# Prompt attention with the keys on partitions: transposed scores 512 queries wide, and no transposes of P

## The chip, the cores and the metric

The kernel runs on one core of one Trainium2 chip. A core has five engines that run side by side, each with an instruction queue of its own that it works off in order: TensorE (PE) for matrix products, VectorE (DVE), ScalarE (ACT), GpSimd (POOL) and SyncE (SP), which issues nearly all DMAs here. A program set the order in each queue when the kernel was built. The metric is the time of one execution on the device in microseconds (us), lower is better.

## The reference

One inference step of a one-layer streaming encoder. 1168 rows go through every dense product: 128 new rows of eight running streams (16 each, with 512 cached rows), and a prompt of 16 learned meta tokens and 1024 frames. Two attentions run in parallel on the same input, a forgetting attention (below: Fox) and a latent one (MLA), 8 heads each; a gated merge and a convolutional feed-forward part follow. What matters here is the attention of the prompt:

```
def attend(q, k, v, bias, scale):
    s = jnp.einsum('bqhd,bkhd->bhqk', q, k).astype(jnp.float32) * scale + bias
    p = jax.nn.softmax(s, axis=-1).astype(v.dtype)
    return jnp.einsum('bhqk,bkhd->bqhd', p, v)
...
fox_bias:  jnp.where(causal, Fq[..., None] - F[:, :, None, :], NEG)   # F: running sum of the log forget values
mla_bias:  cid = jnp.where(idx < N_META, 0, 1 + (idx - N_META) // CHUNK)   # CHUNK = 64
           jnp.where((cid[None, :] <= cq[:, None]) & key_ok[None, :], 0.0, NEG)
```

So for each of 16 heads there are 1024 queries and 1040 keys, causal for Fox and causal by chunks of 64 for MLA. All of it is in float32.

## The kernel before

A float32 product is made of products of two reduced parts: a number x is held as `h` (x rounded to the matrix format, an ACT copy) and `l` (x minus h, a DVE subtraction); the helper `split` (line 293) is this pair of instructions. A dense product takes three matmuls (hh, hl, lh).

The program has these stages in time: projections of all rows; the attention of the running streams; **the attention of the prompt (`sweep`, line 1070)**, from 555 to 943 us of the profiled execution; the merge and the output projection; the feed-forward part, from 1108 us to the end.

In `sweep` a unit is one head and two blocks of 128 queries. Queries are on partitions. `fronts` (line 960) makes the scores of a block in pieces of up to 456 keys, in banks of PSUM named `sb` (two of them). Fox takes two matmuls a piece: high and low parts of k lie one above the other on 128 partitions, q's high part (twice) and low part are the weights. MLA takes three. A bf16 matmul with the identity adds the causal mask `trib` for Fox. `evac_min` (line 667) is one DVE instruction that adds the bias, writes the score to SBUF (`S`) and keeps the row's minimum (scores are negated, so this is softmax's maximum). ACT then takes exp of the row and its sum (line 989), DVE the reciprocal of the sum, one number per query (lines 993 to 1001), and POOL scales the row (lines 994 to 1004).

`backs` (line 1008) turns P around: `lift` puts 128x128 pieces of P through PE transposes into `tb`, `split` brings them to SBUF as `ph` and `pl`, and `pv` multiplies them with V, 256 queries wide, into `ob`. The 16 meta keys are a product of their own (`pm` and `vm`). `finish` adds the two halves of `ob` and stores the head's output (`of`) to DRAM.

`sweep` writes the order of PE out by hand (`emit`, with each piece pinned): the fronts of the next units and pieces of other dense work (`slices`: the gates in Fox, the output projection of Fox in MLA, in banks `mmb`) are spread between the pieces of the present unit. The other queues follow from program order. SBUF tiles for a head's keys and queries are loaded one head ahead, each tile with two buffers.

Of the kernel before, what the change touches and what calls it, by code (L numbers as in the profile page):

```python
# [19 lines left out]
P = 128  # L20
D = 1024
KT = 8
NSMP = 128
# [45 lines left out]
def build(ctx, nc, tc, a):  # L69
# [25 lines left out]
    VF, VM = scratch("VF", [8, P, 1024]), scratch("VM", [8, P, 1024])  # L95
    VZF, VZM = scratch("VZF", [64, 2, 1024]), scratch("VZM", [64, 2, 1024])
# [177 lines left out]
    tri32 = const("tri", [P, P])  # L274
    c16 = const("c16", [P, 16])
    dma(VZF, a["zv"])
    dma(VZM, a["zv"])
    idb = cp.tile([P, P], BF16, name="idb")
    trib = cp.tile([P, P], BF16, name="trib")
    dve.tensor_copy(idb, ident)  # L280
    dve.tensor_copy(trib, tri32)
# [25 lines left out]

    def put_meta(Z, cs, src):
        z4 = Z.rearrange("(g w r) x c -> w x r g c", g=2, w=2)
        for w in range(2):  # L310
            store(z4[w, w][:, :, cs], src.unsqueeze(1).to_broadcast([16, 2, src.shape[-1]]))
# [20 lines left out]
    def fv_tile(i):  # L332
# [14 lines left out]
        put_meta(VZF, cs, f(vmt).rearrange("p h t d -> p (h t d)"))  # L347
        for jq in range(2):
# [7 lines left out]
            store(VF[4 * jq:4 + 4 * jq, :, cs].rearrange("j p c -> p j c"),  # L356
# [76 lines left out]
    with tc.tile_pool(name="rk", bufs=1, side="right") as rk:  # L433
# [37 lines left out]
        for j, (t0, tn) in enumerate(toks[1:]):  # L471
# [11 lines left out]
            if j:  # L483
                store(VM[j - 1], vhl)
            else:
                put_meta(VZM, slice(0, 1024), vhl)

    with tc.tile_pool(name="rm", bufs=1, side="right") as rm:
# [60 lines left out]
        store(FPR, no)  # L549
        ls = rm.tile([64, NK], F32, name="ls")  # L550
# [361 lines left out]
    def head_tiles(kind, h):  # L912
        t = {}
        hs = slice(64 * h, 64 * h + 64)
        fox = kind == 0
        np_ = P if fox else 96
        k1 = pp.tile([np_, NP], F32R, tag="k1", name="k1", padded_shape=[P, NP])
        q1 = pp.tile([np_, NF_], F32R, tag="q1", name="q1", padded_shape=[P, NF_])
        q2 = pp.tile([np_, NF_], F32R, tag="q2", name="q2", padded_shape=[P, NF_])
        if fox:  # L920
            dma(f(k1[0:64]), KFH[hs])
            dma(f(k1[64:128]), KFL[hs])
            for e in range(2):
                dma(f(q1[64 * e:64 * e + 64]), QH[hs])
                dma(f(q2[64 * e:64 * e + 64]), QL[hs])
            fb = pp.tile([P, NP], F32, tag="x", name="fb", padded_shape=[P, NP])
            dma(fb, FPR[h:h + 1, :].to_broadcast([P, NP]))
            t["fb"] = fb
        else:
# [78 lines left out]
    def backs(kind, h, s, t, SS):  # L1008
# [5 lines left out]
        def lift(jp):  # L1014
            def go():
# [11 lines left out]
                if last:  # L1027
                    pe.transpose(tb[0:32, col:col + P], SS[:, 0:32], ident)
# [476 lines left out]
```

## Time and profile before

| | |
|---|---|
| time, median of 3 runs | 1974.3 us (1972.53 to 1976.03) |
| the profiled execution: its own time | 1977.4 us |
| its span in the trace | 1975.6 us |
| span of the prompt's attention | 555 to 943 us |
| mean granted clock of TensorE | 0.993 |

The profile was taken from one execution by the hardware. It gives each instruction's start and duration on its engine, and for idle time the event that ended it. PE's durations overlap, since matmuls are pipelined and their ends are modelled; what one matmul costs in a row is the distance between two starts. DVE's durations overlap a little too: the next instruction's start is about 0.08 us ahead of the end of the one before.

### The profile page before, as it was taken

The page shows a single profiled execution, that of the slowest core. Times are in us where ns is not written, and L with a number is a line of the kernel's source. Part 1 is how long each engine was busy: PE and PEld are TensorE (multiplying, and loading weights), DVE is VectorE, ACT ScalarE, POOL GpSimd, SP SyncE. Part 2 cuts the span into 40 slices and gives each one's busy share as a digit, 9 for nine tenths or more (in the row PEclk, how much of TensorE's full clock was granted, in tenths as well). Part 3 has the DMA queues.
Part 4 walks back from the last instruction along what each step waited for, and adds up shares of the span by engine and source line. Part 5 has one row for each costly group of instructions (what it writes and reads, how often), then busy time and mean ns, then how long its engine had stood idle before and what let it go on. Part 6 is the DMA issues. An engine that isn't in the chain of part 4 may idle for free.

```text
span 1975.6 us, 30184 instructions
## 1 busy us (share of the span) xinstructions
PE 1926.9 (98%) x11766; PEld 1855.5 (94%) x11766; DVE 1125.4 (57%) x2118; ACT 700.0 (35%) x1182; POOL 333.2 (17%) x508
## 2 busy tenths in 40 slices
PE   8999999998999999999999999999999999999997
PEld 7999988988889898999899999999999999999996
DVE  7345355332547777666863465555645655645567
ACT  6222132122446667666632231121221221221235
POOL 5110000111123333333312200000000000000024
PEclk9999999998999999999999999999999999999999
DMA  5345346795576565551733511111111111111112
GB/s 177 115 156 200 132 182 221 243 313 161 180 180 174 143 150 146 123 121 38 243 135 132 185 43 43 43 43 34 42 44 43 43 43 43 34 42 43 43 41 98
DMA packets 112824, 228.07 MB, mean 115 GB/s; under 512 B 12738, under 2 KB 66402, under 8 KB 111626
## 3 DMA queue, kind: packets, MB, share of 16 engines
q1 hardware_dynamic: 112138, 225.62, 37.0%
q8 instruction: 93, 1.52, 0.3%
q10 hardware_dynamic: 544, 0.52, 0.1%
q14 instruction: 49, 0.40, 0.1%
HBM read 165.87 MB, written 61.12 MB: 115 GB/s over the span
## 4 chain that ended last, share of the span: by engine, by line
PE 85%; DVE 6%; DMA 4%; ACT 2%; issue 2%; SPq 1%; POOL 1%; DVEq 0%; ACTq 0%; POOLq 0%
PE nb L63 59%; PE mmb L63 9%; PE ob L63 6%; PE sb L63 6%; PE tb L66 4%; DVE res L1377 1%; PE tb L63 1%; DMA gb<-GL 1%; DVE S L669 1%; DMA wr<-w_a 1%; DMA craw<-cckvT 1%; DVE ga L1189 0%; POOL ss L243 0%; DVE res L1280 0%; DVE zl L295 0%
## 5 line engine op out<-in xcount | busy, mean ns | idle before, releaser
L160 ACT ACTIVATE wh<-wr 128x1024 fp32r<-128x1024 f32 (+3 forms) x131 | 128.5, 981 | 725.2 <-PE nb L63 629.0
L63 PE MATMUL nb<-yl,wh 128*128 128x390 f32 (+1 forms) x1056 | 359.6, 341 | 0.0
L63 PE MATMUL nb<-yh,wl 128*128 128x390 f32 (+1 forms) x1056 | 358.8, 340 | 0.0
L63 PE MATMUL nb<-yh,wh 128*128 128x390 f32 (+1 forms) x1056 | 358.6, 340 | 0.0
L63 PEld LDWEIGHTS nb<-yh,wh 128*128 128x128 f32 x1056 | 199.2, 189 | 0.5
L63 PEld LDWEIGHTS nb<-yl,wh 128*128 128x128 f32 x1056 | 198.8, 188 | 0.4
L63 PEld LDWEIGHTS nb<-yh,wl 128*128 128x128 f32 x1056 | 198.7, 188 | 0.0
L63 PE MATMUL nb<-hh,wh 128*128 128x390 f32 (+2 forms) x552 | 184.3, 334 | 0.0
L63 PE MATMUL nb<-hl,wh 128*128 128x390 f32 (+2 forms) x552 | 183.6, 333 | 0.3 <-DVE hl L295 0.3
L63 PE MATMUL nb<-hh,wl 128*128 128x390 f32 (+2 forms) x552 | 183.5, 332 | 0.0
L1280 DVE TENSOR_TENSOR res<-nb,res 128x390 f32<-128x390 f32 (+3 forms) x260 | 137.2, 547 | 69.1 <-PE nb L63 68.5
L63 PE MATMUL nb<-xh,wh 128*128 128x390 f32 (+1 forms) x480 | 166.3, 346 | 5.4 <-ACT wh L160 5.4
L1261 DVE TENSOR_TENSOR up<-nb,rb 128x390 f32<-128x390 f32 x88 | 49.4, 562 | 205.0 <-PE nb L63 205.0
L63 PE MATMUL nb<-xh,wl 128*128 128x390 f32 (+1 forms) x480 | 164.8, 343 | 0.6 <-DVE wl L161 0.6
L63 PE MATMUL nb<-xl,wh 128*128 128x390 f32 (+1 forms) x480 | 163.7, 341 | 0.2 <-DVE xl L230 0.2
L161 DVE TENSOR_TENSOR wl<-wr,wh 128x1024 fp32r<-128x1024 f32 (+2 forms) x107 | 127.5, 1191 | 45.9 <-ACT wh L160 45.5
L63 PE MATMUL sb<-k,q 96*128 96x456 f32 (+17 forms) x560 | 141.6, 351 | 4.3 <-DVE mx L669 2.7
L295 DVE TENSOR_TENSOR pl<-tb,ph 128x512 fp32r<-128x512 f32 (+1 forms) x160 | 101.5, 634 | 27.6 <-ACT ph L294 25.4
L989 ACT ACTIVATE S<-S,mx 128x400 f32<-128x400 f32 (+7 forms) x128 | 100.5, 786 | 42.5 <-DVE mx L669 41.5
L63 PE MATMUL mmb<-xh,wh 128*128 128x390 f32 (+1 forms) x312 | 110.9, 355 | 0.0
L63 PE MATMUL mmb<-xh,wl 128*128 128x390 f32 (+1 forms) x312 | 106.7, 342 | 1.3 <-POOL wl L161 1.3
L294 ACT ACTIVATE ph<-tb 128x512 fp32r<-128x512 f32 (+1 forms) x160 | 88.1, 551 | 52.1 <-PE tb L66 49.7
(314 smaller groups left out, 4023.9 us busy)
## 6 DMA issues: line engine op xcount, KB each, us to landing
wr<-w_up SPq DMA_DIRECT2D x44, 512.0 KB
wr<-w_a SPq DMA_DIRECT2D x28, 512.0 KB
wr<-w_down SPq DMA_DIRECT2D x22, 512.0 KB
krw<-ckT SPq DMA_DIRECT2D x8, 1024.0 KB
vr<-cv SPq DMA_DIRECT2D x8, 1024.0 KB
GL<-gl SPq DMA_DIRECT2D x26, 195.0 KB
ga<-GL SPq DMA_DIRECT2D x8, 584.0 KB
gb<-GL SPq DMA_DIRECT2D x8, 584.0 KB
```

Of the source, the lines that this page charges most:

```text
L63: return self._put(self.eng.matmul(*args, **kw))
L66: return self._put(self.eng.transpose(*args, **kw))
L160: act.activation(wh[:, sl], wr[:, sl], AF.Copy)
L161: (eng or dve).tensor_tensor(wl[:, sl], wr[:, sl], f(wh[:, sl]), ALU.subtract)
L294: act.activation(hi, src, AF.Copy)
L295: (eng or dve).tensor_tensor(lo, src, f(hi), ALU.subtract)
L669: dve.tensor_tensor_reduce(out=S[:, c0:c1], in0=ps, in1=bias, scale=1.0, scalar=(3.0e38 if prev is None else prev), op0=ALU.add, op1=ALU.m ...
L989: act.activation(S[:, :n], S[:, :n], AF.Exp, bias=mn["m"], scale=-1.0, accum_out=rs[:, i % 2:i % 2 + 1])
L1261: dve.tensor_tensor(up[:, 18 + c0:18 + c1], ps, rb2[:, c0:c1], ALU.mult)
L1280: pin(dve.tensor_tensor(res[:, m, d0:d1], ps, res[:, m, d0:d1], ALU.add))
L1377: pin(dve.tensor_tensor(rm_, rm_, st["v"], ALU.mult))
```

## The change

The prompt's attention is written anew.

- **Scores are transposed.** Keys are on partitions, in 9 blocks of 128 (the last one padded with zeros), and queries are the wide side, up to 512. A head has two halves of 512 queries; half 0 has 5 blocks of keys, half 1 has 9, together 14 pieces. A piece needs no transposes: its exp is already the operand that `pv` takes. The meta keys are part of block 0.
- **The row minima come from a pass by query** (`fronts`). A softmax with keys on partitions can't take a maximum along partitions, so the scores are made a second time by query, with one matmul a piece and in banks `tb`, only for DVE's minimum; its elementwise output is thrown away (`junk`, bf16). `low` splits the 8 minima of each partition into two parts, `rows` transposes them and DVE spreads them (16 x 1024) into rows 96 to 111 of the tile `q2`. Against rows of ones in `k1` they are subtracted by the score matmul itself.
- **Fox's bias by key** is ACT's bias in the exp (`nfk`, made once); the masks are added by bf16 matmuls for both kinds.
- **Row sums**: POOL adds the pieces of P up elementwise (`acc`), 12 additions a head; at the end of a half `acc` is split and multiplied with ones, which gives each query's sum on 64 partitions. DVE takes the reciprocal of that (64 x 512), and POOL multiplies the output with it.
- `split` of P now reads SBUF (`pt`) on both engines; before, it read PSUM.
- V is loaded with the meta rows in front, so some small DMAs and zero tiles of the old layout are gone. Tiles of a head are in two fixed sets; a set is loaded again when its head is done.
- The order is written anew: scores of piece u, with pieces of the next head's fronts from u = 6 on; `pv` two pieces later; the sums' product three pieces after a half's end.

```
-                    ps = sbank()[:, :L]
-                        pe.matmul(ps, t["q1"][:, qs], t["k1"][:, c0:c1], start=True, stop=False)
-                        pe.matmul(ps, t["q2"][:, qs], t["k1"][:, c0:c1], start=False, stop=not lastc)
...
-                    mn["m"] = evac_min(S, ps, bias, c0, c1, mn["m"], pp)
-                    if lastc:
-                        act.activation(S[:, :n], S[:, :n], AF.Exp, bias=mn["m"], scale=-1.0,
-                                       accum_out=rs[:, i % 2:i % 2 + 1])
...
+                    ps = tbank()[:, :L]
+                    if kind == 0:
+                        pe.matmul(ps, t["q1"][:, qs], t["k2"][:, c0:c1], start=True, stop=not lastc)
...
+                    else:
+                        pe.matmul(ps, t["q1"][0:96, qs], t["k1"][0:96, c0:c1], start=True, stop=True)
...
+                    dve.tensor_tensor_reduce(out=junk[:, :L], in0=ps, in1=bias, scale=1.0,
+                                             scalar=(3.0e38 if mn["m"] is None else mn["m"]),
+                                             op0=ALU.add, op1=ALU.min, accum_out=m)
...
+        def low():
+            m2 = pp.tile([P, 16], F32R, tag="m2", name="m2")
+            act.activation(m2[:, 0:8], mins, AF.Copy, scale=-1.0)
+            dve.scalar_tensor_tensor(m2[:, 8:16], mins, -1.0, f(m2[:, 0:8]), ALU.mult, ALU.subtract)
...
+        def rows():
+            tb = tbank()
+            pe.transpose(tb[0:16, 0:P], f(st["m2"]), ident)
+            dve.tensor_tensor(t["q2"][96:112, :].rearrange("r (b q) -> r b q", b=8),
+                              tb[0:16, 0:P].unsqueeze(1).to_broadcast([16, 8, P]),
+                              d16.unsqueeze(2).to_broadcast([16, 8, P]), ALU.mult)
...
-                        pe.transpose(tb[:, col:col + P], S[:, ks], ident)
...
-                split(tb[:, :col], ph[:, :col], pl[:, :col])
...
+        for half in range(2):
+            q0 = 512 * half
+            jl = 8 if half else 4
+            for j in range(jl + 1):
+                cl = max(q0, P * j - back)
+                n = q0 + 512 - cl
...
+                    ps = sbank()[:, :n]
+                    if fox:
+                        pe.matmul(ps, k2[:, ks], q1[:, qs], start=True, stop=False)
+                    else:
+                        pe.matmul(ps, k1[0:96, ks], q1[0:96, qs], start=True, stop=False)
+                        pe.matmul(ps, k2[0:96, ks], q1[0:96, qs], start=False, stop=False)
+                    mask = m1 > m0
+                    pe.matmul(ps, k1[:, ks], q2[:, qs], start=False, stop=not mask)
...
+                    if fox:
+                        act.activation(pt, ps, AF.Exp, bias=nfk[:, j, h:h + 1], scale=-1.0)
+                    else:
+                        act.activation(pt, ps, AF.Exp, scale=-1.0)
+                    ph = pp.tile([P, 512], F32R, tag="ph", bufs=3, name="ph")
+                    pl = pp.tile([P, 512], F32R, tag="pl", bufs=3, name="pl")
+                    split(pt, ph[:, :n], pl[:, :n])
+                    if j:
+                        sm_ = st["acc"][:, cl - q0:]
+                        pool.tensor_tensor(sm_, sm_, pt, ALU.add)
...
+                def sums(st=st):
+                    ah = pp.tile([P, 512], F32R, tag="ph", bufs=3, name="ah")
+                    al = pp.tile([P, 512], F32R, tag="pl", bufs=3, name="al")
+                    split(st["acc"], ah, al)
...
+                def finish(st=st, q0=q0):
+                    ah, al = st["a"]
+                    rs = tbank()
+                    pe.matmul(rs, onesr, ah, start=True, stop=False)
+                    pe.matmul(rs, onesr, al, start=False, stop=True)
+                    ob = st["ob"]
+                    ot = pp.tile([64, 512], F32, tag="ot", bufs=1, name="ot")
+                    act.activation(ot, ob[64:128], AF.Copy)
+                    of = pp.tile([64, 512], F32, tag="of", name="of")
+                    dve.tensor_tensor(of, ob[0:64], ot, ALU.add)
+                    rv_ = pp.tile([64, 512], F32, tag="rvs", bufs=1, name="rvs")
+                    dve.reciprocal(rv_, rs[0:64])
...
+                    pool.tensor_tensor(of, of, rv_, ALU.mult)
```

Two places show the new order. The first is DVE's queue. Before, in the middle of the Fox heads (`pl` and `pm` are the low parts of the turned P, `ri` the reciprocals per query, the ISA rows the minimum pass):

```order
L295 TENSOR_TENSOR pl<-tb,ph 128x384
L997 RECIPROCAL ri<-rs 128x2
L1036 TENSOR_TENSOR pm<-tb,pm 32x128
L1064 TENSOR_TENSOR of<-ob,ot 64x256
L669 ISA S,mx<-sb,fb 128x328
L669 ISA mx 128x1
L295 TENSOR_TENSOR pl<-tb,ph 128x512
```

Now, at the border of two MLA heads (the first two rows bring the minima of the next head into `q2`, `al` is the low part of the last half's sums, the rows `pl` belong to the next head's half 0, `rvs` and `of` to the last head's half 1):

```order
L1005 SCALAR_TENSOR_TENSOR m_8642<-mins,m_8642 128x8
L1011 TENSOR_TENSOR q_0_5078<-tb,c_d_585 16x1024
L297 TENSOR_TENSOR al<-acc,ah 128x512
L297 TENSOR_TENSOR pl<-acc,ph 128x512
L297 TENSOR_TENSOR pl<-pt,ph 128x448
L1087 RECIPROCAL rvs<-tb 64x512
L297 TENSOR_TENSOR pl<-pt,ph 128x320
L1085 TENSOR_TENSOR of<-ob,ot 64x512
L297 TENSOR_TENSOR pl<-pt,ph 128x192
L297 TENSOR_TENSOR pl<-pt,ph 128x64
```

The reciprocal was one or two columns wide and is 512 wide; the subtractions read PSUM before and read two SBUF tiles now; and the spreading of the minima stands between two heads.

The second place is POOL's queue. Before, in the Fox heads (all but the last row scale P by `ri`):

```order
L999 TENSOR_SCALAR S<-S,ri 128x144
L1003 TENSOR_SCALAR S<-S,ri 128x16
L1004 TENSOR_SCALAR S<-S,ri 128x256
L994 TENSOR_SCALAR S<-S,ri 128x656
L161 TENSOR_TENSOR wl<-wr,wh 128x1024
```

Now, from half 0 of a Fox head on:

```order
L1059 TENSOR_TENSOR acc<-acc,pt 128x400
L1059 TENSOR_TENSOR acc<-acc,pt 128x272
L1059 TENSOR_TENSOR acc<-acc,pt 128x144
L1059 TENSOR_TENSOR acc<-acc,pt 128x16
L1092 TENSOR_TENSOR of<-of,rvs 64x512
L1059 TENSOR_TENSOR acc<-acc,pt 128x512 x3
```

POOL's operations on one tile have become operations on two, and the multiplication that waits for DVE's reciprocal stands between the additions.

## Rows read from the trace of the kernel before

**Rows 1.** The page, part 1: busy us (share of the span) and instructions of each engine

```profile
PE 1926.9 (98%) x11766; PEld 1855.5 (94%) x11766; DVE 1125.4 (57%) x2118; ACT 700.0 (35%) x1182; POOL 333.2 (17%) x508
```

**Rows 2.** Windows: stretch, length, busy us (instructions) of PE PEld DVE ACT POOL, clock, DMA

```profile
555.00:943.00 388.00, 380.09 (x2578) 346.11 (x2577) 274.37 (x858) 252.63 (x589) 130.33 (x203) 0.99 0.53 134
```

**Rows 3.** The same stretch, instructions on mmb alone: busy of PE PEld DVE ACT

```profile
555.00:943.00 388.00, 114.28 (x546) 94.64 (x545) 7.25 (x13) 10.19 (x21) 0.99 0.53 134
```

**Rows 4.** Timeline of PE at two places: start us, duration us, instruction

```profile
602.12 0.34 PE L63 MATMUL mmb<-xh,wl 128*128 128x390 f32 x1
602.30 0.28 PE L63 MATMUL ob<-ph,v 128*128 128x256 f32 x1
602.41 0.28 PE L63 MATMUL ob<-pl,v 128*128 128x256 f32 x1
...
602.77 0.60 PE L66 MATMUL tb<-c_ident,S 128*128 128x128 f32 x4
603.12 0.36 PE L63 MATMUL ob<-ph,v 128*128 128x256 f32 x1
...
300.38 0.40 PE L63 MATMUL nb<-wh,cl 128*128 128x512 f32 x1
300.61 0.39 PE L63 MATMUL nb<-wl,ch 128*128 128x512 f32 x1
```

**Rows 5.** Waits of PE, 545 to 955 us, longest first: total us, times, longest

```profile
PE sb L63 <- DVE mx L669: 2.7, 4, 1.3
```

**Rows 6.** Lines by form, DVE, 555 to 943 us: busy us, mean ns, idle before

```profile
L295 DVE TENSOR_TENSOR pl<-tb,ph 128x512 fp32r<-128x512 f32 x96 | 65.9, 686 | 6.2 <-ACT ph L294 5.2
L295 DVE TENSOR_TENSOR pl<-tb,ph 128x384 fp32r<-128x384 f32 x64 | 35.6, 556 | 21.4 <-ACT ph L294 20.2
L1064 DVE TENSOR_TENSOR of<-ob,ot 64x256 f32<-64x256 f32 x56 | 23.1, 413 | 7.9 <-ACT ot L1058 5.6 <-DMA OML<-of 1.1
L1036 DVE TENSOR_TENSOR pm<-tb,pm 32x128 fp32r<-32x128 f32 x64 | 17.9, 280 | 11.1 <-ACT pm L1035 9.1
L1001 DVE RECIPROCAL ri<-rs 128x1 f32<-128x1 f32 x32 | 5.2, 163 | 17.4 <-ACT S L989 17.4
```

**Rows 7.** Lines by form, DVE, 335 to 339 us

```profile
L534 DVE RECIPROCAL d__2738<-d__2738 128x73 f32<-128x73 f32 x1 | 0.6, 615 | 0.0
L535 DVE TENSOR_TENSOR e<-e,d__2738 128x73 f32<-128x73 f32 x1 | 0.2, 236 | 0.0
```

**Rows 8.** Timeline of POOL and DVE in the merge

```profile
999.32 2.85 POOL L1184 TENSOR_TENSOR ga<-ga,ya 128x1168 f32<-128x1168 f32 x1 [3.59 <-ACT ga L1182]
...
999.50 1.03 DVE L1188 TENSOR_TENSOR gb<-nb,gb 128x390 f32<-128x390 f32 x2
1000.63 2.76 DVE L1189 TENSOR_TENSOR ga<-ga,gb 128x1168 f32<-128x1168 f32 x1
1003.32 1.21 DVE L161 TENSOR_TENSOR wl<-wr,wh 128x1024 fp32r<-128x1024 f32 x1
...
1007.34 1.38 DVE L1189 TENSOR_TENSOR ga<-ga,gb 128x1168 f32<-128x1168 f32 x1
```

**Rows 9.** Lines by form, POOL, 555 to 943 us

```profile
L161 POOL TENSOR_TENSOR wl<-wr,wh 128x512 fp32r<-128x512 f32 x8 | 10.3, 1285 | 3.1 <-ACT wh L160 3.1
L1004 POOL TENSOR_SCALAR S<-S,ri 128x512 f32<-128x512 f32 x16 | 11.1, 695 | 0.0
```

**Rows 10.** Lines by form, ACT, 555 to 943 us

```profile
L1035 ACT ACTIVATE pm<-tb 32x128 fp32r<-32x128 f32 x64 | 16.7, 261 | 21.2 <-DVE pl L295 21.1
L989 ACT ACTIVATE S<-S,mx 128x528 f32<-128x528 f32 x16 | 11.7, 728 | 0.5 <-DVE mx L669 0.5
L160 ACT ACTIVATE wh<-wr 128x512 fp32r<-128x512 f32 x9 | 5.7, 630 | 2.7 <-PE mmb L63 2.7
```

**Rows 11.** Windows at the start of the prompt's attention, columns as in rows 2

```profile
560.00:565.00 5.00, 3.10 (x13) 1.69 (x14) 2.15 (x9) 1.55 (x4) 0.00 (x0) 0.90 1.10 290
565.00:570.00 5.00, 4.89 (x19) 3.99 (x19) 3.20 (x13) 2.35 (x4) 2.56 (x4) 0.50 1.05 217
```

More of the change, by code (lines that the diff above doesn't have):

```diff
@@ new lines, in build @@
+    sets = []
+    for i in range(2):
+        t = {"k1": pp.tile([112, NKP], F32R, bufs=1, name=f"k1_{i}"),
+             "k2": pp.tile([P, NKP], F32R, bufs=1, name=f"k2_{i}"),
+             "q1": pp.tile([P, NF_], F32R, bufs=1, name=f"q1_{i}"),
+             "q2": pp.tile([112, NF_], F32R, bufs=1, name=f"q2_{i}"),
+             "v": pp.tile([P, 9, P], F32R, bufs=1, name=f"v_{i}")}
+        pool.memset(f(t["k1"][:, NP:]), 0.0)
+        pool.memset(f(t["k1"][64:96, :NP]), 0.0)
+        pool.memset(f(t["k1"][96:112, :]), 1.0)
+        pool.memset(f(t["k2"][:, NP:]), 0.0)
+        pool.memset(f(t["q2"][64:96, :]), 0.0)
+        pool.memset(f(t["v"][:, 8, :]), 0.0)
+        sets.append(t)
@@ L923, in head_tiles @@
+    mz = pp.tile([P, NP], F32, bufs=1, name="mz")
+    onesr = pp.tile([P, P], F32R, bufs=1, name="onesr")
+    act.activation(onesr, ones, AF.Copy)
+    def head_tiles(idx):
+        kind, h = idx // H, idx % H
+        t = sets[idx % 2]
+        k1, k2, q1, q2, v = (t[n] for n in ("k1", "k2", "q1", "q2", "v"))
+        hs = slice(64 * h, 64 * h + 64)
+        if kind == 0:
+            dma(f(k2[0:64, :NP]), KFH[hs])
+            dma(f(k2[64:128, :NP]), KFL[hs])
             for e in range(2):
@@ L950, in chunks, with head_values, fronts @@
+    def head_values(idx):
+        kind, h = idx // H, idx % H
+        v = sets[idx % 2]["v"]
+        V = VM if kind else VF
+        cs = slice(h * P, (h + 1) * P)
+        dma(f(v[:, 0:8, :]), V[0:1024, cs].rearrange("(j p) c -> p j c", p=P))
+        dma(f(v[0:16, 8, :]), V[1024:NP, cs])
+    def fronts(idx):
+        kind = idx // H
+        t = sets[idx % 2]
+        mins = pp.tile([P, 8], F32, tag="mins", name="mins")
         out = []
-        for i in (2 * s, 2 * s + 1):
+        for i in range(8):
@@ L1103, in emit @@
                 fn()
-        mean = [sum(cost for s_ in SORD for _, _, _, cost in chunks(k_, s_)) / 10 for k_ in range(2)]
-        open_unit()
-        open_unit()
-        open_unit()
+        for i in range(2):
+            head_tiles(i)
+            head_values(i)
         filler(F2, True)
-        emit(*take(upto=1)[1])
+        parts, low, rows = fronts(0)
+        for n_, p_ in enumerate(parts):
+            emit(p_)
+            if n_ % 2:
+                filler(0.8, True)
+        low()
+        filler(2.0, True)
+        emit(rows)
         pend = []
-        for u, (kind, h, s) in enumerate(units):
-            if u == 4 * H:
+        kept = []
+        NU = 14
+        for idx in range(2 * H):
+            if idx == H:
                 emit(*[fn for _, fn in fill])
                 del fill[:]
-                emit(*pend)
+                for _, fn in pend:
+                    emit(*fn)
                 pend = []
@@ L1155, in sweep @@
+            if nxt[2]:
+                emit(nxt[2])
+            if idx + 2 < 2 * H:
+                head_tiles(idx + 2)
+        for _, fn in pend:
+            emit(*fn)
         emit(*[fn for _, fn in kept])
```

302 lines of the change are left out of this document (115 added, 187 removed).

## Prediction

> **What bounds the kernel now.** I read the page's first part, then busy times by stretch, then PE's waits, then lines by form of the other engines. The page shows PE busy for 98% of the span and DVE for 57% [rows 1]: so PE sets the time, and the question is whether it still does in the changed stage. In the stretch of the prompt's attention PE is busy for 380.1 of 388 us, DVE for 274.4, ACT for 252.6, POOL for 130.3 [rows 2]. The longest sum of PE's waits there is 2.7 us, for DVE's minimum [rows 5]. So DVE has about 110 us to spare, 7 us a head, and nothing more. All that the change adds to DVE is to be held against those 7 us.
>
> **PE: what it removes and adds.** A matmul costs the distance between two starts: 0.18 us for 390 columns, 0.11 for 256, 0.23 for 512, and four transposes 0.35 [rows 4]. The other dense work in the stretch is 546 matmuls on `mmb` [rows 3], 546 x 0.18 = 98 us, and stays. So attention costs PE 380 - 98 = 282 us now, 17.6 a head. After the change, a pass over the keys has 4736 columns for Fox and 5120 for MLA, counted from the diff (six pieces of 512, eight narrower). Fox makes two passes for scores, two for `pv`, and one of 4736 for the minima; MLA three, two and one; sums add 4 x 512. That is 25,728 and 32,384 columns. At 512 per 0.23 us they take 11.6 and 14.5 us. Masks and pieces under 256 columns, which won't go below some 0.1 us each, add about 2.5 us (an estimate from the 0.11 us of 256 columns). Eight heads of 14.1 and eight of 17.0 are 249 us, with the dense work 347: 33 us less than 380, and 21.7 a head. The transposes, the meta products and half-width `pv` are the gain. PE alone would take the kernel to about 1941.
>
> **DVE: removed.** Per head 6 + 4 `pl` from PSUM (6 x 0.686 + 4 x 0.556), 4 `pm` x 0.280, 4 `of` x 0.413, 6 reciprocals x 0.163 [rows 6]: 10.1 us in 20 instructions. Neighbours overlap by 0.08 us, so 8.5 us go. The minimum pass stays: the same 14 pieces a head, from PSUM.
>
> **DVE: added.** The two forms of `pl` give 1.02 ns a column and 0.165 us an instruction [rows 6]. I use this line for all plain operations. Per head: 14 `pl` of 4736 or 5120 columns, 7.3 us on average; 2 `al` of 512, 1.4; 2 `of` of 512, 1.35; the spreading of minima, 1024 columns, 1.2; the small subtraction in `low`, 0.24, like the 73 columns in [rows 7]. The reciprocal is another matter. One column takes 0.163 us [rows 6], 73 columns take 0.615, where a multiplication of 73 columns takes 0.236 [rows 7]. That is 6.3 ns a column, six times a plain operation, and partitions don't count. 512 columns are then 0.163 + 511 x 6.3 ns = 3.4 us, two a head 6.7 us. Together 18.2 us in 22 instructions, 16.5 after overlap. The bounds of the reciprocal are 0.69 us (if only fixed cost were longer) and 4.3 us (512/73 of 0.615). I take 3.4, since the two rows of reciprocals fix a fixed part and a slope.
>
> DVE so goes from 274.4/16 = 17.1 to 17.1 - 8.5 + 16.5 = 25.1 us a head, 402 us in all, when it never waits. That is more than the 388 us of the whole stretch now [rows 2], and more than PE's 347. DVE becomes the bound, and PE's 33 us turn into waits.
>
> The Trainium skill, "VectorE: DVE Perf Modes" (section on the 8-slice pipeline), says that the reciprocal is an iterative division with a repeat count of 8. At eight cycles of the 0.96 GHz that the page gives, 512 columns would be an estimated 4.3 us plus the fixed part, 2 us a head more than I count, about 2100 in all; the row of 73 columns, 0.615 us with its fixed part, lies under that rule.
>
> **DVE: its waits.** Two kinds are new.
>
> *The border of heads.* The minima of the next head go from DVE to ACT (0.26 us as the 32x128 copy), back to DVE, through a PE transpose and to DVE for the spreading; only a narrow `pl` lies beside that, so DVE idles about 0.6 us. Then the first scores need `q2`: PE 0.23, ACT's exp 0.73, ACT's copy 0.63 [rows 4, 10] stand between the spreading and the first `pl` of the head, 1.7 us with semaphores, of which `al` covers 0.6. DVE idles 1.1. Behind the waiting `pl` stand the second `pl` and the reciprocal of the last half, and PE's `pv` waits for them. Together 1.7 us a head; nothing if `pv` of the old head and dense pieces kept DVE fed, but by the order DVE has no other instruction there.
>
> *POOL's additions.* In the merge a DVE multiplication of two SBUF tiles takes 1.38 us alone, and 2.76 when it starts 1.3 us into a POOL operation of 2.85 us on two SBUF tiles [rows 8]; it ends 1.2 us after POOL's does. It has waited for POOL to end, and the 2.76 holds that wait. Now `pl` reads PSUM and one tile, and POOL works on one tile (0.70 us for 512 columns). After the change `pl` and `al` read two SBUF tiles, and POOL's additions too, 1.285 us for 512 columns [rows 9], 2.5 ns a column. POOL adds 3712 or 4096 columns a head and multiplies 1024: 12.4 us. If POOL is busy for 12.4 of 29 us and the rest of the one met is 0.5 us, 16 subtractions lose 16 x 0.43 x 0.5 = 3.4 us. Less, since POOL can go on while DVE is in its 6.7 us of reciprocals, from PSUM. I take 2.7. The bounds are 0 and about 12.8 (every `pl` meets the addition of its own piece, which may start one ACT copy earlier, 16 x 0.8).
>
> The Trainium skill, "SBUF — State Buffer" (section on the two separate sides), states the same as a rule: DVE with two SBUF inputs and GpSimd take a shared pair of ports in turn, and the loser waits for the whole instruction. The trace agrees (2.76 against 1.38 us). Without the rule the sum would be 16 x 2.7 = 43 us lower.
>
> **The sum.** A head takes 25.1 + 1.7 + 2.7 = 29.5 us, 16 heads 472 us. The first head's minimum pass is in it, but DVE idles there between PE's pieces, some 5 us. The last half's reciprocal and POOL's multiplication (3.4 + 1.3 us) are covered by the six kept pieces of dense work, 36 x 0.18 us. With the 5 us ahead of the first score, as now, the stretch goes from 388 to 482, 94 us more. ACT: per head 14 exps, 14 copies, and four more of 512, about 20 us by [rows 10]: under 29.5, no bound. POOL 12.4 and 1.3 for weights: no bound. DMA: about 2 MB a head, as now, and 134 GB/s in the stretch now [rows 2]: hidden. Before the stage, small DMAs go and ten small transposes come, under 2 us either way, hidden under the running streams' dense work. The profiled execution took 1977.4 us, 2071 with 94 us more; the median is 3 us lower. I predict 2070.
>
> **Rivals.**
>
> *DVE fits under PE, and the kernel gets faster: 1941.* The place is the 64x512 reciprocal. If it cost 1.6 us or less, DVE's 25.1 would fall to 21.6, PE's own 21.7 a head; from there PE decides, and with the two waits hidden the whole 33 us come out. For it: the slope rests on one instruction of 73 columns. Against: that one costs 2.6 times a plain operation of its width, and even with a cheap reciprocal the border and POOL's additions would have to be hidden. 7%, and 3% for a tie near the present time.
>
> *DVE bound without waits: 2000 to 2040.* POOL's additions fall into the reciprocals and the borders overlap with other DVE work. 402 + 5 + 5 us against 388 gives 1998, the lower end of this case. Against: the order puts the reciprocal behind the first two `pl`, so the gap at the border stays. 20%.
>
> *The waits are larger, and PE's clock falls: 2105 to 2180.* Where PE was busy for 3.1 of 5 us at the start of this stage, the granted clock fell, and in the next 5 us it was 0.50, the 1.2 GHz level [rows 11]. In my forecast PE is busy for 21.7 of 29.5 us, with gaps at each reciprocal and border. If it ran at 0.75 on average, PE would need 29 us a head and no longer catch up between DVE's waits. At 33 us a head the stretch takes 538 us, and the kernel 2124. For it: two waits of over 2 us a head. Against: PE has 8 us of slack a head. 22%.
>
> My forecast, 2040 to 2105, has 48%. The range of 2008 to 2135 holds it, most of the case without waits and half of the case with a falling clock. Slower by over 0.2% (what this measurement can tell from no change) is the sum of three cases, 90%.
>
> **What would show it.** Right: DVE busy for over 85% of the stage at about 400 us; reciprocals of 64x512 at 3.4 us, 32 of them; `pl` from SBUF with a mean well over 0.165 + 1.02 ns x columns, with POOL's `acc` beside the long ones; PE's waits in the stage going from under 3 us to some 100 us, behind `pl`, the minima and `q2`; nothing moved before 555 us or after the merge. Wrong: reciprocals under 2 us, or PE still busy for 95% of the stage.

## The result, and the profile after

The changed kernel takes 2187.1 us (median of 4 runs, 2182.5 to 2188.5) against 1975.2 (1972.5 to 1976.1): ratio 1.1072, 95% interval 1.1051 to 1.1092. The direction was forecast (slower, 90%), the size was not: 212 us more in place of 95, above the range's 2135. The profiled execution took 2186.5 us with a span of 2184.3. Part 1 of its page, against [rows 1]:

```profile
PE 2006.4 (92%) x11279; PEld 1879.8 (86%) x11279; DVE 1309.4 (60%) x2086; ACT 728.6 (33%) x1169; POOL 455.6 (21%) x553
```

PE executes 487 instructions less and is busy for 80 us more, at a lower share. Windows show where (columns as in [rows 2]; the first row is what lies ahead of the first head's scores, the second the 15 heads after it, from one spreading of minima to the next, the third the last head):

```profile
555.00:583.00 28.00, 26.81 (x170) 24.23 (x168) 9.55 (x34) 3.17 (x8) 9.44 (x13) 1.00 0.85 200
583.00:1114.00 531.00, 411.38 (x1862) 328.09 (x1862) 417.20 (x768) 260.01 (x533) 221.75 (x219) 0.84 0.36 88
1114.00:1155.00 41.00, 34.81 (x177) 29.68 (x177) 31.24 (x33) 24.76 (x50) 18.04 (x16) 0.96 0.16 46
```

Read the second row per head, as fifteenths: 35.4 us, PE busy for 27.4, DVE for 27.8, the granted clock 0.84 on average between its levels of 1.2 and 2.4 GHz (0.5 and 1.0). No engine is near full. The forecast had 29.5 us a head: DVE busy for 27.8 with its waits for POOL, idle for 1.7. So DVE's work came out to the tenth; what it lacks is 7.6 us of idle time, not 1.7. Lines by form of DVE, 555 to 1155 us, answer to [rows 6, 7]:

```profile
L1087 DVE RECIPROCAL rvs<-tb 64x512 f32<-64x512 f32 x32 | 106.9, 3342 | 0.1
L297 DVE TENSOR_TENSOR pl<-pt,ph 128x512 fp32r<-128x512 f32 x64 | 72.9, 1141 | 5.1 <-ACT ph L296 4.7
L297 DVE TENSOR_TENSOR al<-acc,ah 128x512 fp32r<-128x512 f32 x32 | 25.8, 807 | 7.6 <-ACT ah L296 7.4
L297 DVE TENSOR_TENSOR pl<-acc,ph 128x512 fp32r<-128x512 f32 x32 | 24.4, 764 | 35.8 <-ACT ph L296 35.4 <-PE sb L63 0.4
L1011 DVE TENSOR_TENSOR q<-tb,c_d 16x1024 fp32r<-16x1024 f32 x16 | 19.5, 1217 | 7.4 <-PE tb L66 7.4
```

The reciprocal takes 3.34 us (forecast 3.4), the spreading 1.22 (1.2). `pl` of 512 columns from `pt` takes 1.14 us where it was 0.69 from PSUM (from `acc`, the first piece of a half, 0.76). The fourth row holds the largest idle time: the first `pl` of a half. Waits of PE and then of DVE in the same stretch (us, times, longest); before, the longest sum of PE's was 2.7 us [rows 5]:

```profile
PE tb L63 <- DVE rvs L1087: 40.7, 15, 5.1
PE ob L63 <- DVE pl L297: 29.0, 20, 3.1
PE tb L63 <- DVE mins L994: 16.9, 29, 1.4
PE sb L63 <- DVE q L1011: 13.1, 14, 1.3
PE tb L66 <- DVE m L1005: 12.6, 9, 2.2
```

```profile
DVE pl L297 <- ACT ph L296: 55.9, 52, 4.9
DVE junk L994 <- PE tb L63: 35.7, 39, 2.3
```

PE waits for DVE and DVE for PE (through ACT's `ph`, or directly with `junk`, the minimum pass): over the 15 heads PE is idle for 120 us and DVE for 114. Ahead of the stage, too, PE has a new wait, 300 to 360 us:

```profile
PE tb L66 <- DVE no L543: 11.5, 1, 11.5
```

These are the nine small transposes that the change adds for `nfk`. They stand in PE's queue behind DVE's scan, which waits for a DMA. The last copy of the running streams starts at 553.9 us, 9.4 later than before.

One head border on DVE, the one with the most idle time of the 15 (start, duration, instruction):

```profile
1006.41 0.69 DVE L297 TENSOR_TENSOR al<-acc,ah 128x512 fp32r<-128x512 f32 x1 [0.61 <-ACT ah L296]
1007.02 0.16 DVE L1005 SCALAR_TENSOR_TENSOR m<-mins,m 128x8 fp32r<-128x8 f32 x1
1007.55 1.22 DVE L1011 TENSOR_TENSOR q<-tb,c_d 16x1024 fp32r<-16x1024 f32 x1 [0.37 <-PE tb L66]
1012.72 0.69 DVE L297 TENSOR_TENSOR pl<-acc,ph 128x512 fp32r<-128x512 f32 x1 [3.96 <-ACT ph L296]
1016.03 0.63 DVE L297 TENSOR_TENSOR pl<-pt,ph 128x448 fp32r<-128x448 f32 x1 [2.62 <-PE tb L63]
1016.58 3.34 DVE L1087 RECIPROCAL rvs<-tb 64x512 f32<-64x512 f32 x1
```

Four waits, 7.6 us, where the forecast had two of 1.7 together. Between them on PE stand the scores, six dense matmuls that began 0.32 us apart instead of 0.18, and six more. The 15 borders, counted from `al` to the reciprocal as here, have 3.9 us of idle time on average, 58 of DVE's 114 us; of the rest, along the heads, 32 us are waits of the minimum pass.

### The profile page after: what moved, and what is told of

It is laid out like the page before. It is cut to its first block, busy times and chain, and to the rows that moved or that the text cites. A ratio compares the mean times of both kernels' runs of the same rounds, so it can differ in the third digit from the quotient of the medians.

```text
span 2184.3 us, 29336 instructions
## 1 busy us (share of the span) xinstructions
PE 2006.4 (92%) x11279; PEld 1879.8 (86%) x11279; DVE 1309.4 (60%) x2086; ACT 728.6 (33%) x1169; POOL 455.6 (21%) x553
## 4 chain that ended last, share of the span: by engine, by line
PE 76%; DVE 13%; issue 5%; ACT 3%; DMA 2%; POOL 1%; SPq 0%; DVEq 0%; ACTq 0%; POOLq 0%
PE nb L63 54%; PE mmb L63 9%; PE sb L63 5%; PE ob L63 4%; PE tb L63 3%; DVE rvs L1087 2%; DVE pl L297 2%; DVE junk L994 2%; PE tb L66 1%; DVE q L1011 1%; DMA ga<-GL 1%; DVE res L1402 1%; ACT ph L296 1%; POOL acc L1059 0%; DVE zl L297 0%
## 5 line engine op out<-in xcount | busy, mean ns | idle before, releaser
L1059 POOL TENSOR_TENSOR acc<-acc,pt 128x400 f32<-128x400 f32 (+2 forms) x192 | 178.7, 931 | 275.9 <-ACT pt L1051 103.8
L63 PE MATMUL sb<-q,k 96*128 96x512 f32 (+14 forms) x560 | 162.8, 388 | 14.2 <-DVE q L1011 13.1
L297 DVE TENSOR_TENSOR pl<-pt,ph 128x400 fp32r<-128x400 f32 (+2 forms) x192 | 144.7, 763 | 28.2 <-ACT ph L296 20.4
L63 PE MATMUL tb<-k,q 128*128 128x144 f32 (+13 forms) x224 | 90.5, 437 | 64.4 <-DVE rvs L1087 40.7
L63 PEld LDWEIGHTS sb<-q,k 96*128 96x128 f32 (+2 forms) x560 | 111.2, 217 | 34.6 <-DVE q L1011 18.8
L63 PEld LDWEIGHTS tb<-k,q 128*128 128x128 f32 (+1 forms) x224 | 50.8, 231 | 87.2 <-issue 35.9
```

Source lines behind the costliest of these rows:

```text
L63: return self._put(self.eng.matmul(*args, **kw))
L297: (eng or dve).tensor_tensor(lo, src, f(hi), ALU.subtract)
L1059: pool.tensor_tensor(sm_, sm_, pt, ALU.add)
```

## The experiments

All are edits of the changed kernel, each timed against the kernel before on the same chip; a difference is taken from its 2187.1 us.

### The priced terms: reciprocal and additions

```
-                    dve.reciprocal(rv_, rs[0:64])
+                    dve.tensor_copy(rv_, rs[0:64])
```

> The changed kernel (2187 us) with the 64x512 reciprocal replaced by a plain copy of the same tile on the same engine (so nothing is divided). DVE has 32 x (3.34 - 0.68) = 85 us less to do. If DVE's work and its own waits set the stage, the time falls by about those 85 us, to 2102. Theory clock (PE at 1.2 GHz in a good part of the stage is what the forecast missed): the waits of PE behind the reciprocal go too, the granted clock of the stage rises from about 0.8 to over 0.9, and the time falls by more, to 2050-2085. Theory chain (head border, buffers and PE's queue set the time, DVE only waits less often on paper): under 60 us come out, over 2127.

2103.4 us (ratio 1.0653, 1.0636 to 1.0670), 84 less. The copy takes 0.68 us, so 85 us of DVE's work went and came out one to one: DVE's work is on the path. The clock of the 15 heads rose from 0.84 to 0.88, and no more than those 84 us came out (their stretch, columns as in [rows 2]):

```profile
579.00:1040.00 461.00, 389.55 (x1865) 312.48 (x1863) 342.01 (x769) 258.40 (x534) 224.11 (x219) 0.88 0.42 101
```

The additions left out:

```
-                        pool.tensor_tensor(sm_, sm_, pt, ALU.add)
-                    split(st["acc"], ah, al)
+                    act.activation(ah, st["acc"], AF.Copy, bias=1.0)
+                    dve.tensor_tensor(al, st["acc"], f(ah), ALU.add)
```

> The changed kernel without GpSimd's additions of pieces into the row sum (the divisor is a stand-in made of the first piece). POOL then has no work on two SBUF tiles beside DVE's pl. Measured excess of pl and al over their rows from PSUM is some 57 us. Theory clock: pl back at 0.69 us for 512 columns, and 57 us or more come out: 2100-2130. Theory chain: part of the excess lay beside other waits, 20-40 us come out: 2147-2167; the ACT copy ah and the minima's copy behind it no longer wait for POOL, some 0.5 us a head of this.

2160.7 us (1.0948, 1.0929 to 1.0966), 26 less: the second theory. `pl` of 512 columns fell to a mean of 0.91 us only, since 16 of the 64 still took 0.75 us or more, each beside a POOL instruction, 15 times its multiplication. How they meet, from the changed kernel:

```profile
669.17 1.27 POOL L1092 TENSOR_TENSOR of<-of,rvs 64x512 f32<-64x512 f32 x1 [0.44 <-DVE rvs L1087]
```

```profile
665.75 3.34 DVE L1087 RECIPROCAL rvs<-tb 64x512 f32<-64x512 f32 x1
669.02 0.36 DVE L994 CUSTOM_DVE_ANT_0 junk<-tb,fb 128x264 bf16<-128x264 f32 x1
669.31 0.07 DVE L994 DVE_READ_ACCUMULATOR2_ANT mx<- 128x1 f32 x1
669.31 1.67 DVE L297 TENSOR_TENSOR pl<-pt,ph 128x512 fp32r<-128x512 f32 x1
```

POOL's multiplication starts when the reciprocal has ended; DVE has one piece of the minimum pass to do before `pl`. So POOL starts first and ends at 670.44; `pl` ends 0.54 us after that, at 670.98. Of the 64 such `pl` in the changed kernel 50 took 0.75 us or more, and each of the 50 overlaps a POOL instruction. This is the rule of the Trainium skill, "SBUF — State Buffer" (the two separate sides), that the loser of the shared ports waits for the whole instruction. The trace agrees: `pl` took 1.67 us in place of 0.69, and ended only after POOL did.

Both edits at once:

> The copy in place of the reciprocal and no additions on GpSimd at once (nothing is divided, and the row sum is that of the first piece). Alone the one took 84 us out and the other 26. Theory clock: with both, PE is near its own bound, the granted clock passes 0.93, and more than the sum comes out: 2040-2065. Theory consequence or chain: the sum or less, 2077-2100.

2053.0 us (1.0389, 1.0367 to 1.0410): 134 less, where the two alone add up to 110. The clock of the 15 heads is 0.94. The first theory's range held it. The 24 us beyond the sum fit that theory too, but no run says how much of them is the clock and how much are waits.

### Waits and buffers one by one

Four buffers in place of three:

```
-                    ph = pp.tile([P, 512], F32R, tag="ph", bufs=3, name="ph")
+                    ph = pp.tile([P, 512], F32R, tag="ph", bufs=4, name="ph")
... and the same for pl, ah, al
```

> The changed kernel with four buffers each for ph (with ah) and pl (with al) instead of three. At one border the first ph of a head waited 1.7 us for PE's pv of the piece before the last, which stood behind six dense matmuls. Theory buffers (the missing DVE idle at the border, some 2 us a head, is this reuse): 25-40 us come out, 2147-2162. Theory chain without buffers (PE reaches that pv late anyway, and the next wait takes its place): under 10 us, 2177-2190.

2195.6 us (1.1112, 1.1084 to 1.1139): nothing gained, and a little slower than either theory had it. The minima's high part by DVE:

```
-            act.activation(m2[:, 0:8], mins, AF.Copy, scale=-1.0)
+            dve.tensor_scalar(m2[:, 0:8], mins, -1.0, None, ALU.mult)
```

> The changed kernel with the high part of the minima made by DVE itself, not by ACT behind its copy ah, which waits for POOL's last addition. The chain from the last minimum to the transpose loses a semaphore each way and 0.2-0.9 us. Theory chain: 0.5-0.9 us a head come out where PE stands (12.6 us of PE's waits are for this m), 8-15 us, 2172-2179. Theory DVE (DVE's own work and idle elsewhere decide): within 4 us of 2187, since DVE gets 0.16 us a head more.

2183.1 us (1.1045, 1.1012 to 1.1078): 4 less, and the intervals overlap. The `tb` bank freed early:

```
-                    dve.reciprocal(rv_, rs[0:64])
+                    act.activation(rv_, rs[0:64], AF.Copy)
+                    dve.reciprocal(rv_, rv_)
```

> The changed kernel with the sums copied by ACT from PSUM to SBUF (0.6 us) before the reciprocal, which then stays 3.3 us long on DVE but no longer holds one of the two T banks. PE waited 40.7 us in the stage for this bank. Theory bank: PE runs ahead with the minimum pass during the reciprocal, DVE then finds its work ready, and 20-40 us come out: 2147-2167. Theory chain or clock without the bank: PE's wait of 40.7 us goes, but turns into waits for DVE elsewhere; under 8 us: 2179-2190.

2193.4 us (1.1101, 1.1073 to 1.1129), above both ranges. PE no longer waits for `rvs`, but now 37.5 us for the minimum pass on the same banks; PE's largest wait only changed its name:

```profile
PE tb L63 <- DVE mx L994: 37.5, 19, 3.3
```

### PE's work and its clock

Less work for PE, the low product cut to 64 columns of each piece:

```
-                    pe.matmul(o, v[:, j, :], pl[:, :n], start=False, stop=(j == jl))
+                    w = min(n, 64)
+                    pe.matmul(o[:, n - w:], v[:, j, :], pl[:, n - w:n], start=False, stop=(j == jl))
```

> The changed kernel with the product of the low parts of P with V cut to the last 64 columns of each piece (so the output lacks most of that correction); every wait and every instruction of DVE, ACT and POOL stays. PE loses some 3900 columns a head, 1.75 us at 2.4 GHz, 3.5 at 1.2. Theory clock (PE at half clock is co-bound in the stage): 2-3 us a head, 30-50 us come out, 2137-2157. Theory chain of waits (PE's speed is a small part): under 12 us, 2175-2190.

2196.3 us (1.1106, 1.1072 to 1.1140): no gain, above both ranges. By the expectation this would make PE's speed a small part; the trace shows why it can't be read so. Over the 15 heads PE was busy for as long as before (412 us), with less to do, at a clock of 0.80 instead of 0.84. The twelfth head, where the two differ most, in the changed kernel and then in this one (windows, columns as in [rows 2]):

```profile
975.20:1007.50 32.30, 25.48 (x131) 21.06 (x130) 27.82 (x51) 17.96 (x38) 16.40 (x15) 0.95 0.43 98
```

```profile
968.70:1004.80 36.10, 29.11 (x130) 24.30 (x129) 28.47 (x52) 18.17 (x38) 14.84 (x15) 0.80 0.38 88
```

Clock 0.95 with 32.3 us, 0.80 with 36.1; which of the two brings the other about, this pair does not tell. No dense pieces between the heads' matmuls:

```
-                sl = slices(share)
+                sl = []
...
-        emit(*[fn for _, fn in kept])
+        emit(*[fn for _, fn in fill + kept])
```

> The changed kernel with no dense pieces between the attention's own matmuls: those of the first eight heads stand in one block before head 8, the others after the last head; all work is done. The 546 dense matmuls take 98 us at 2.4 GHz in blocks. Theory clock: PE alone is under half busy within a head, its clock stays at 0.5 there, a head still takes 34-37 us, and the kernel 2230-2285. Theory chain with dense pieces as its part (pieces stand in PE's queue ahead of scores that DVE and ACT wait for): a head falls to 29-31 us, and the kernel takes 2150-2200.

2259.4 us (1.1448, 1.1431 to 1.1465): all heads but the first, and the one with the dense block, still take 33.7 to 36.5 us. The time, and nearly all heads, are in the clock theory's ranges; the clock is not: 0.63 to 0.77 in place of 0.5. The heads take about as long at some 0.7 as they do at 0.84 with the dense work between, so this run does not show what the clock costs. Seven useless matmuls at each border, where PE waits:

```
+            ob = obank()
+            for _ in range(7):
+                pe.pin()
+                pe.matmul(ob, t["k1"][0:96, 0:P], t["q1"][0:96, 0:512], start=True, stop=True)
... (the bank goes on to the next head's first product)
```

> The changed kernel with seven matmuls of 512 columns more at each of 16 head borders, in PE's queue just ahead of the transpose of the minima, where PE waits for about 1.9 us; their results are overwritten. At 2.4 GHz they take 7 x 0.23 = 1.6 us, 26 us of work in all. Theory clock: the clock no longer falls at the border (the dense matmuls behind it start 0.18 us apart, not 0.32), the stage's granted clock rises by 0.05 or more, and the time falls by 15-40 us in spite of the added work: 2147-2172. Theory chain: the same time or slower, 2185-2215, at a higher granted clock.

2195.4 us (1.1126, 1.1106 to 1.1145), clock 0.86: as the chain had it. Useless matmuls in every piece:

```
+    act.activation(zr, ones, AF.Copy, scale=0.0)
...
+                    for _ in range(2):
+                        pe.pin()
+                        pe.matmul(o, zr, ph[:, :n], start=False, stop=False)
```

> The changed kernel with two matmuls more per piece, in PE's queue between the two products with V: they add zero (weights of zero times ph) to the output's bank, 2 x 4928 columns a head, 4.4 us at 2.4 GHz, 70 us of added PE work in all. They stand where PE waits for pl. Theory clock (PE's gaps let the clock fall, and attention at 1.2 GHz is what lengthens a head; in the changed kernel heads of granted clock 0.90-0.95 take 32.3-34.7 us, those of 0.74-0.80 take 36-40): the granted clock of the stage rises from 0.84 to 0.90 or more, a head falls from 35.4 to 33-34 us, and the kernel takes 2145-2175, faster with more work. Theory consequence (the clock falls because PE waits, and costs nothing): 2187 or slower, up to 2257.

> The same with four such matmuls per piece: 8.8 us a head at 2.4 GHz, 140 us in all. PE alone then needs some 30.5 us a head at full clock. Theory clock: granted clock 0.95 or more, a head 31-33.5 us, the kernel 2120-2165. Theory consequence: 2220-2330.

Two per piece: 2188.7 us (1.1078, 1.1052 to 1.1103); four: 2221.2 (1.1243, 1.1219 to 1.1267). 70 us of added PE work cost nothing, 140 us cost 34. Both times lie at the lower end of the consequence theory's ranges, and neither in the clock theory's. The halves of the stage tell more. The changed kernel's first eight heads (Fox) and last seven, and the same with two zeros per piece:

```profile
582.80:862.50 279.70, 210.72 (x948) 165.51 (x948) 216.58 (x409) 133.69 (x269) 113.39 (x115) 0.83 0.38 93
862.50:1114.10 251.60, 200.96 (x916) 162.68 (x916) 200.81 (x359) 126.52 (x264) 108.46 (x104) 0.85 0.35 82
```

```profile
582.10:850.50 268.40, 221.73 (x1173) 180.34 (x1172) 217.65 (x410) 134.73 (x269) 114.02 (x115) 0.94 0.39 96
850.50:1113.10 262.60, 220.37 (x1108) 183.07 (x1107) 204.10 (x361) 127.98 (x265) 107.61 (x104) 0.93 0.34 79
```

The Fox heads became faster with more work, the MLA heads slower. So the zeros were put into the Fox heads alone (`range(2 if fox else 0)`):

> The changed kernel with the two matmuls of zeros per piece only in the first eight heads (Fox), whose granted clock was lowest: 8 x 4736 x 2 columns more, 34 us of PE work at 2.4 GHz. With zeros in all heads the first eight took 268 us in place of 280, the last seven 12 us more. Theory clock (PE at 1.2 GHz lengthens those heads by itself): the kernel is faster than 2187 with more work, 2170-2180. Theory consequence (the clock costs nothing; the 12 us were chance): 2187 or slower, up to 2221.

2178.1 us (1.1026, 1.1009 to 1.1044), 9 less with 34 us more work for PE, in the clock theory's range; the interval lies below that of the changed kernel. The two halves:

```profile
582.70:854.90 272.20, 226.35 (x1174) 184.01 (x1172) 218.63 (x410) 134.36 (x269) 113.63 (x115) 0.92 0.39 95
854.90:1105.00 250.10, 198.10 (x916) 160.69 (x915) 200.03 (x360) 126.52 (x264) 109.83 (x104) 0.86 0.35 83
```

Only the first half changed: clock 0.83 to 0.92, 7.5 us less. So these heads became faster with more work for PE, in two runs (268.4 and 272.2 us in place of 279.7). That the low clock costs time of its own is the likely reading; it isn't shown, since the zeros also shift when PE's next instructions start, and in the MLA heads a clock of 0.93 in place of 0.85 didn't pay for the added work. How much the clock costs in all stays open, since no edit changes it alone.

### The border, and what PE needs alone

The minimum pass two pieces earlier, its rows ahead of the last piece's scores:

```
-                want = 0 if u < 6 else min(len(todo), -(-len(todo) // max(1, 13 - u)) if u < 13 else len(todo))
+                want = 0 if u < 4 else min(len(todo), -(-len(todo) // max(1, 11 - u)) if u < 11 else len(todo))
-                if u == 12 and nxt[1]:
+                if u == 10 and nxt[1]:
                     nxt[1]()
-            if nxt[2]:
-                emit(nxt[2])
+                if u == 12 and nxt[2]:
+                    emit(nxt[2])
```

> The changed kernel with the minimum pass of the next head two pieces earlier (pieces 4 to 10 of 14, not 6 to 12), its minima's transpose and spreading ahead of the last piece's scores instead of behind them. Theory border: DVE's wait for the first two ph of a head was 50 to 65 us in every kernel so far, whatever the clock and DVE's load, 3.5 us a head where the forecast had 1.7 in all; with the spread minima ready before the head ends, 2 to 3.5 us a head come out and the kernel takes 2130-2155. Theory elsewhere (the wait is only where DVE happens to stand when it has nothing; the minimum pass crowds into fewer pieces and the T banks): the same 2187 within 10 us.

2161.3 us (1.0937, 1.0910 to 1.0964), 26 less, between the two theories: DVE's wait for `ph` over the 15 heads fell from 52.2 to 29.1 us, that for PE's minimum pass stayed (32.2 and 28.5); the changed kernel and then this one:

```profile
DVE pl L297 <- ACT ph L296: 52.2, 49, 4.9
DVE junk L994 <- PE tb L63: 32.2, 35, 2.3
```

```profile
DVE pl L297 <- ACT ph L296: 29.1, 43, 2.4
DVE junk L994 <- PE tb L63: 28.5, 37, 2.6
```

The reciprocal by ACT, with the minima's high part by DVE, without and with the earlier pass:

```
-                    dve.reciprocal(rv_, rs[0:64])
+                    act.activation(rv_, rs[0:64], AF.Ln)
+                    act.activation(rv_, rv_, AF.Exp, scale=-1.0)
```

> All work done: the reciprocal as exp(-ln x) by two ACT instructions of 64x512 (0.5-0.6 us each, the tables are loaded already), and the high part of the minima by DVE. DVE has 107 us less than the changed kernel, 22 less than with the copy (2103); ACT gets 19 us and is busy for half the stage. Theory clock: DVE's 22 us and a higher clock come out beyond the copy, 2065-2090. Theory chain: ACT's two instructions stand ahead of exps in its queue and give it back, 2095-2110.

> All work done: the earlier minimum pass with the reciprocal as exp(-ln x) by ACT and the minima's high part by DVE (2095 us without the earlier pass). Theory border: 2 to 3.5 us a head come out, 2040-2063, and the granted clock of the stage rises from 0.90 to 0.94 or more. Theory elsewhere: 2085-2105.

2095.5 us (1.0599, 1.0571 to 1.0627), at the fast end of the chain theory's range, and 2073.5 (1.0494, 1.0465 to 1.0523), again between the two. ACT's two instructions take 0.59 and 0.63 us. The second is the fastest variant that does all the work. The copy in place of the reciprocal, no additions and the earlier pass together:

> The earlier minimum pass in the kernel with a copy for the reciprocal and no additions on GpSimd (2053 us; nothing is divided, and the row sum is that of the first piece). All three terms of the loss are then gone: DVE has some 20 us a head, PE 21.7. Theory (the three terms and the clock that follows them are the whole loss): PE decides again, the clock stays above 0.97, and the kernel comes near the kernel before, 1975-2010. Theory elsewhere: 2035-2060.

2029.1 us (1.0265, 1.0234 to 1.0296): with all three terms out still 55 us above the kernel before, between the two theories. Last, DVE's `pl` out as well:

```
-                    split(pt, ph[:, :n], pl[:, :n])
+                    act.activation(ph[:, :n], pt, AF.Copy)
...
-                    pe.matmul(o, v[:, j, :], pl[:, :n], start=False, stop=(j == jl))
+                    pe.matmul(o, v[:, j, :], ph[:, :n], start=False, stop=(j == jl))
```

> The kernel of the earlier minimum pass with a copy for the reciprocal and no additions on GpSimd (2029 us), and now without pl either: the second product with V takes ph again (the output has no low part, no division, and a row sum of the first piece alone). PE's work is the same in columns and instructions; DVE falls to some 13 us a head. It measures what PE alone needs in this layout, which the forecast put at 21.7 us a head and the kernel at 1941. Theory coupling (PE's sum was right, and what was missed is that DVE, ACT and PE, each in order, do not run beside each other without loss): 1935-1955. Theory PE (the sum for PE was too low, at 24-25 us a head with dense work): 1970-2000.

2001.4 us (1.0136, 1.0119 to 1.0153), just above the range of the theory on PE's sum. Its 15 heads, then its Fox heads and six MLA heads:

```profile
583.00:948.00 365.00, 339.26 (x1861) 279.26 (x1858) 199.46 (x560) 254.79 (x531) 52.38 (x39) 0.98 0.52 128
583.40:767.10 183.70, 168.64 (x944) 136.40 (x944) 104.76 (x295) 127.98 (x264) 25.82 (x19) 0.98 0.56 138
801.30:948.00 146.70, 143.37 (x806) 122.47 (x805) 75.13 (x217) 105.22 (x222) 23.10 (x18) 1.00 0.49 112
```

In the MLA heads PE is busy for 98% at full clock: 24.5 us a head. Fox heads take 23.0, with PE busy for 21.1. Over all 15 a head takes 24.3 us, with PE busy for 22.6: a little more work than the 21.7 of the forecast, and 1.7 us of idle time even now. DVE still has 13.3 us a head and ACT 17.0, so this is not PE all alone. But with half of DVE's load out, and nearly at full clock, the layout is still slower than the kernel before.

### The wait ahead of the stage

The nine transposes and their two copies moved to just ahead of the first head's rows, from a tile loaded from `FPR`:

```
+    no2 = pp.tile([H, NP], F32, bufs=1, name="no2")
+    dma(no2, FPR)
...
         filler(2.0, True)
+        tb = tbank()
+        ... the nine transposes of no2, the two copies to nfk
         emit(rows)
```

> The changed kernel with the nine small transposes of the summed forget gates (and their two copies) moved from the projections, where PE waits 11.5 us for DVE's scan at about 340 us, to just ahead of the first head's rows; the scanned row is loaded again from DRAM there. Theory wait (PE's queue stood still for 11.5 us ahead of the stage, and the running streams end 9.4 us later for it): 8-11 us come out, 2176-2179, and the copies of the running streams end near 545 us as in the kernel before. Theory cover (the dense work that stood behind is only done elsewhere, and the stage is no earlier): within 4 us of 2187.

2183.4 us (1.1055, 1.1039 to 1.1071). The wait is gone, and the running streams' last copy starts at 544.6 us, 9.3 earlier; at the ninth head's border the kernel is still 9 us ahead (897.0 against 906.0). At the last border it is 5 ahead: the twelfth head, which had a clock of 0.95, has 0.85 now (35.3 us in place of 32.3). So the wait delayed the stage as expected; of the whole time only 4 us is measured, and the intervals overlap, which is the other theory's number.

## Why the prediction was wrong

**Right.** The price of the reciprocal, from its two rows [rows 6, 7]: 3.34 us for 3.4. Here the Trainium skill, "VectorE: DVE Perf Modes" (the 8-slice pipeline), with its repeat count of 8, read as eight cycles a column, would have given an estimated 4.3. The measurement decides against that reading, at (3342 - 163)/511 = 6.2 ns a column. DVE's work is on the path: the 85 us of the reciprocal came out one to one. DVE's busy time came out at 27.8 us a head, as forecast, but partly by luck, as two errors cancel. The excess of `pl` and `al` over 0.165 us + 1.02 ns a column, POOL's port, is 57 us in sum or 3.6 a head (2.7 forecast; out of the time came 26 alone). DVE's own work is then 24.2, not 25.1. (The list of what DVE loses has 24 instructions and not 20, so that 8.2 us go and not 8.5; 5 us in all.)

**The failed step: DVE's waits, put at 1.7 us a head because "PE has 8 us of slack a head".** The sum of 25.1 + 1.7 + 2.7 let DVE wait at the border and nowhere else. Measured are 7.6 us: 3.9 at the border and 3.7 along the head, where the sum had nothing, 2.1 of them at the minimum pass. That is 5.9 us a head more, over the 15 heads 89 of the 117 missing us. Another 18 lie ahead of the first head: from 555 us to its first scores it takes 28 us, where I had 10. Two things are behind the waits.

*PE's own sum.* "PE alone would take the kernel to about 1941" came from columns at 512 per 0.23 us and a flat 2.5 us for narrow pieces and masks. The kernel with half of DVE's work out takes 2001, 60 us more. A head takes 24.3 us there in place of 21.7, 39 of the 60 us; of the 2.6, PE's busy time is 0.9 and its idle time 1.7. Less its dense matmuls (27 and 35 a head at 0.18 us) attention is 16.2 us in a Fox head and 17.6 in an MLA head, where I had 14.1 and 17.0. So of a head of 29.5 us 5 are left for slack, not 8. The gain on PE that the change was given, 33 us, isn't there: even this kernel is 27 us slower than the one before.

*The engines do not run beside each other without loss.* I added up DVE's busy time and two waits and took PE for hidden. But PE, ACT and DVE work off their queues in order and hand each piece around, so DVE waits wherever PE is late, and PE the other way; the rows of waits show both. Half of DVE's idle time is at the borders, and the earlier minimum pass, which puts the spreading ahead of the last piece's scores, gave 26 us back. What the rest comes from is not settled: four buffers for `ph` and `pl`, the bank and the minima's split changed nothing one by one, more banks for the scores were not tried, and two loads taken out together gave 24 us more than apart.

**The clock, a rival at 22%.** It fell as that rival said, to 0.84, and PE's slack went with it: 27.4 us busy a head. Its price of 33 us a head was still low, and 2187 lies above its range too. The zeros in the Fox heads speak for a clock that costs time of its own; its share of the 89 us is open.

**"Nothing moved before 555 us."** Wrong: the small transposes that I hid under dense work (ten in the forecast, nine of them these) stand in PE's in-order queue, and the dense work stands behind them. The stage starts 9.4 us later; of the whole time at most some 4 us is measured.

**The signs.** Of those named, the reciprocals came true, and so did the long `pl` and PE's waits of over 100 us. DVE is busy for 79% of the 15 heads, not for over 85%, and that is the sign that tells of the miss.

Taken out one after the other, the loss reads: reciprocal 84 us (2187 to 2103), additions 50 with it (2053), the border 24 (2029), the rest of DVE's `pl` 28 (2001), and 27 that are left (against 1974 on the same chip). Each figure holds in this order only. No variant beats the kernel before.

## What to carry to other kernels

When a change brings two engines close to each other (here 27.8 and 21.7 us a head in the forecast), don't hide the smaller one: count the hand-overs in a period and expect idle time on both (here 7.6 and 8.0 us of 35.4). A sum for the engine that is to be relieved needs the same care as that for the one that is loaded; measure it with the other's work left out. Work can't cover an instruction that waits for another engine if it stands behind it in the same queue (here nine small transposes, 11.5 us of waiting).

## What the runs showed of the hardware

PE's work can shrink or grow by some us a head without changing the time, with the granted clock going the same way. With 1.75 us a head less to do (at 2.4 GHz) the 15 heads had a clock of 0.80 instead of 0.84 and took as long; with 4.4 us more they had 0.94 and took as long; and with 34 us of useless matmuls in the Fox heads, their clock at 0.92 in place of 0.83, the kernel was 9 us faster. So taking work out of PE and timing the kernel does not show whether PE is on the path.
